# A hybrid trunk step on one core: unread products and another split order at the head, late state adds, output in one tensor, one output block by two products

## The chip, the cores and the metric

The kernel runs on one core of a Trainium2 chip. The metric is the device time of one execution in microseconds (us). Each kernel is run several times, and the median counts. The times and the profile are of the program as it runs on the chip; what the host does with the arrays before and after is not in them.

The engines are named as in the profile: PE is TensorE (the matrix products; PEld its weight loads), ACT is ScalarE, DVE is VectorE, POOL is GpSimd, and SP is SyncE, whose queue issues most of the DMAs.

## The reference

One layer (`DEPTH = 1`) of a model step for two request groups that share the weights: 256 new positions of a prompt and 32 positions of a running stream, 288 rows together, with 2048 features.

```python
def run_layer(...):
    xn = rmsnorm(x, norm_mix_pre)
    proj = xn @ w_in            # [u_pool 1024 | z 2048 | xBC 2560 | dt 32]
    pool = pool_mixer(u_pool)   # trailing means over 2, 4, 8, 16 positions
    ssd  = ssd_mixer(z, xBC, dt)  # causal conv, Mamba-2 scan, gate, norm; returns the new state
    x    = x + rmsnorm(concat[pool, ssd] @ w_out, norm_mix_post)
    h    = rmsnorm(x, norm_ffn_pre)
    up   = causal_dwconv3(h @ w_up)            # 2 * 5632 columns
    x    = x + rmsnorm((silu(gate) * value) @ w_down, norm_ffn_post)
```

The outputs are y for the prompt and for the sample, and for both groups the new pool history, the new conv histories and the new SSD state. The data type is fp32. A product with the unit matrix or with a diagonal matrix therefore stands for a copy or a scaling by rows.

## The kernel before

Activations lie with the features on the partitions: a tile is 128 features by 288 positions (`NT`; columns 0 to 255 are the prompt, 256 to 287 the sample). Every fp32 weight product is made of three faster products (`mm3`, L136 to L138): ACT copies a weight tile `raw` into a rounded `whi`, DVE subtracts it from `raw` and writes the remainder `wlo`; the activations are split in the same way (`xn`, `hn` and so on, by `split_from`, L99 on ACT and L100 on DVE). Weights come in by SP's queue, a few buffers ahead.

The order of the instructions comes from a scheduler that places the engines' queues. `keep_in_program_order` pins an instruction to its place in the program, `issue_after` sets it behind a given one, `high_priority` lets the fetches and splits run ahead.

The stages, in order of time:

- **The head** (L235 to L290). The first projection takes 16 k-steps of 128 input features with `w_first`, six output tiles (`acc` five times, `acc_x` once), 18 products a step. For each k the split `xn` of the input, `whi` (L270) and `wlo` (L271) are issued, and `input_squares` (L230 to L234) squares the input on ACT and sums it on POOL (`xsum`). The squares of several tiles go out in the later steps. At k = 13, `input_rstd` (L240) makes the mean over the features by a product with `mean` (a matrix filled with 1/2048), and `root` (L236) takes ACT's square root and DVE's reciprocal.
- **The projections, the SSD scan, the pool and the output projection.** `mix_out` (L660) reads each finished tile twice on ACT: `msq` (L668) the square for the norm, `mg` (L670) the scaled copy. Two last products `psum_m` (L745) end the norm's sum. Behind them come four pinned state updates: `state_s` for j = 3 and 2 (one product `psts`, ACT's copy `sx`, a POOL add into `sh`, L714, and the DMA to `new_ssd_s`), and `state_p` for j = 3 and 2 (two products `pst` each, L701).
- **The up loop** (L773 on). `residual` makes the tile x1[k] on DVE (`mg`, L764), `hn` is its split, and 7 output tiles take 21 products a k-step with `w_up1` (`whi` L798, `wlo` L799). From k = 4 on, the weight split is set behind the split of `hn` of the same k. DVE's work of this loop stands in one line (`in_line`). At k = 15, behind the second output tile, `psum_t` (L806) sums the squares for the next norm and `root` makes `r2`.
- **The feed-forward halves and the end.** Finished tiles of the last projection go through DRAM into rows of positions (`to_tokens`). The last 256 features come last and run in two parts (`run_a` for positions 128 to 287, `run_b` for 0 to 127). `fsq` (L960) are their squares, `psum_f` (L931 to L937) sums over the features, `final_rstd` (L943) takes the root `rf`, `turn` transposes the last tiles on PE. `y_out(q, b)` (L963) makes one block of 128 positions by 512 features of y on DVE: x = ft · rf + x, and writes it. Blocks with b = 1 are written first, then the sample's block `xr_s` (L1042, L1044), then the four blocks with b = 0, whose squares end last.

The sample's block lies in `xr_s` with the quarter q of the features on the partitions 32q to 32q + 31, and goes out as a pattern of 4 x 32 x 512:

```python
sp.dma_start(out=y_sample[0].rearrange("s (q c) -> q s c", q=4), in_=xr_s)
```

Of the kernel before, what the change touches and what calls it, by code (L numbers as in the profile page):

```python
# [43 lines left out]
def body(  # L44
# [16 lines left out]
    w_down,  # L61
    y_prompt,
    y_sample,
    new_pool,
# [180 lines left out]
    act.dma_start(out=g_mix_pre, in_=g0_in)  # L245
    input_tiles(0, 1)
    first = [acc_ps.tile([P, NT], F32, tag="acc", name="acc") if m < 5 else aux([P, NT], "acc_x") for m in range(6)]
    chunks = ((0, 1), (1, 1)) + tuple((k, 2) for k in range(2, KD, 2))
    x_with = {0: (1, 1), 1: (2, 2), 2: (4, 2), 4: (6, 3), 6: (9, 3), 8: (12, 4)}
    for kb, n in chunks:  # L250
        raw = wpool.tile([P, n, 768], F32, tag="raw", name="raw")
        sp.dma_start(out=raw, in_=w_first[:, kb : kb + n, :])
        if kb in x_with:
            input_tiles(*x_with[kb])
        if kb == 1:
            pool.dma_start(out=wdt, in_=w_dt)
        if kb == 2:
            pool.dma_start(out=par1, in_=par1_in)
            pool.dma_start(out=hp, in_=hp_in)
        if kb == 6:  # L260
            pool.dma_start(out=pc, in_=par2_in[:, :120])
            pool.dma_start(out=pf, in_=par2_in[:, 120:].rearrange("p (r t) -> p r t", r=6))
        for k in range(kb, kb + n):
            a = atile("xn")
            split_from(a, xT[:, k, :], g_mix_pre[:, k : k + 1])
            xn.append(a)
            hi, lo = wtile("hi", 1, 768)[:, 0, :], wtile("lo", 1, 768)[:, 0, :]
            step = 256 if k == 0 else 768
            for c in range(0, 768, step):
                act.activation(hi[:, c : c + step], raw[:, k - kb, c : c + step], AF.Copy)  # L270
                dve.tensor_tensor(  # L271
                    lo[:, c : c + step], raw[:, k - kb, c : c + step], hi[:, c : c + step].bitcast(F32), op=ALU.subtract
                )
# [434 lines left out]
    def state_s(j, x, h, pin=False):  # L708
        st = acc_ps.tile([P, 512], F32, tag="acc", name="psts")
        ins = pe.matmul(st, btok[:, j // 2, 2, :], x[:, 2, :], start=True, stop=True)  # L710
        if pin:
            tc.keep_in_program_order(ins)
        act.activation(x[:, 2, :], st, AF.Copy)
        pool.tensor_tensor(h, h, x[:, 2, :], op=ALU.add)  # L714
        sp.dma_start(out=new_ssd_s[:, 512 * j : 512 * j + 512], in_=h)

# [10 lines left out]
    for grp in ((0, 1), (2,), (3,), (4,), (5,), (6,), (7,)):  # L727
# [4 lines left out]
        if 2 <= grp[0] < 4:  # L732
            x_h = state_in(grp[0] - 2)
            state_p(grp[0] - 2, *x_h)
            state_s(grp[0] - 2, *x_h)
        elif 4 <= grp[0] < 6:
            late_in[grp[0] - 2] = state_in(grp[0] - 2)
# [6 lines left out]
    for i in range(2):  # L744
        tc.keep_in_program_order(pe.matmul(p_m, mean, last_sq[i], start=False, stop=i == 1))  # L745
    state_s(3, *late_in[3], pin=True)
    state_s(2, *late_in[2], pin=True)
    state_p(3, *late_in[3], pin=True)
# [23 lines left out]
    for k in range(KD):  # L772
# [190 lines left out]
    def y_out(q, b):  # L963
# [3 lines left out]
        for o, n, src in (  # L967
# [4 lines left out]
            if b:  # L972
                tc.keep_in_program_order(ins)
        sp.dma_start(out=y_prompt[0][b * P : (b + 1) * P, 512 * q : 512 * (q + 1)], in_=x)

# [67 lines left out]
    )  # L1043
    sp.dma_start(out=y_sample[0].rearrange("s (q c) -> q s c", q=4), in_=xr_s)  # L1044
# [12 lines left out]

_OUTS = [
    (1, 256, 2048), (1, 32, 2048), (P, 2, 15, NU), (P, 2, 3, NXC), (P, D_SSD), (P, D_SSD), (P, 2, 2, 2 * NF),
]  # L1060
# [72 lines left out]
```

## Time and profile before

| what | us |
|---|---|
| median of 3 runs | 1330.14 (1330.11 to 1331.14) |
| the profiled execution | 1329.91, span 1328.2 |
| PE busy | 1310.4 (99%) |
| DVE busy | 884.6 (67%) |
| ACT busy | 666.3 (50%) |
| POOL busy | 215.0 (16%) |
| mean granted TensorE clock | 0.997 |

The span runs from the first to the last instruction. Products are pipelined: the record of one lasts longer than the distance to the next. A row of the timeline gives the start, the busy time, the engine, the line, the operation, the tile written and the tiles read, the number of instructions in the row, and in brackets the idle time before it with the one who ended it. A row of the waits gives who waited for whom, the total, the number of times and the longest.

### The profile page before, as it was taken

The page shows a single profiled execution, that of the slowest core. Times are in us where ns is not written, and L with a number is a line of the kernel's source. Part 1 is how long each engine was busy: PE and PEld are TensorE (multiplying, and loading weights), DVE is VectorE, ACT ScalarE, POOL GpSimd, SP SyncE. Part 2 cuts the span into 40 slices and gives each one's busy share as a digit, 9 for nine tenths or more (in the row PEclk, how much of TensorE's full clock was granted, in tenths as well). Part 3 has the DMA queues.
Part 4 walks back from the last instruction along what each step waited for, and adds up shares of the span by engine and source line. Part 5 has one row for each costly group of instructions (what it writes and reads, how often), then busy time and mean ns, then how long its engine had stood idle before and what let it go on. Part 6 is the DMA issues. An engine that isn't in the chain of part 4 may idle for free.

```text
span 1328.2 us, 25077 instructions
## 1 busy us (share of the span) xinstructions
PE 1310.4 (99%) x10041; PEld 1295.1 (98%) x10041; DVE 884.6 (67%) x1460; ACT 666.3 (50%) x1002; POOL 215.0 (16%) x353
## 2 busy tenths in 40 slices
PE   7999999999999999999999999999999999999997
PEld 7999999999999989999999999999999999999996
DVE  8898998779644478977666643345666666664444
ACT  7558777446443455645445443334444444454442
POOL 6221102121211100211111100001111111101110
PEclk9999999999999999999999999999999999999998
DMA  7668884465666445666454454455444544566663
GB/s 287 230 194 255 287 242 160 140 240 206 232 206 207 147 143 195 199 188 185 164 183 162 151 175 161 160 180 177 172 159 164 186 159 159 175 235 175 209 181 93
DMA packets 104008, 249.81 MB, mean 188 GB/s; under 512 B 63748, under 2 KB 69444, under 8 KB 81492
## 3 DMA queue, kind: packets, MB, share of 16 engines
q1 hardware_dynamic: 101972, 243.11, 55.8%
q0 software_dynamic: 1488, 4.92, 1.1%
q8 instruction: 78, 1.28, 0.4%
q14 instruction: 38, 0.31, 0.1%
q10 hardware_dynamic: 432, 0.19, 0.1%
HBM read 236.23 MB, written 11.95 MB: 187 GB/s over the span
## 4 chain that ended last, share of the span: by engine, by line
PE 98%; DVE 1%; DMA 0%; ACT 0%; issue 0%; DVEq 0%; SPq 0%
PE acc L138 31%; PE acc L136 31%; PE acc L137 31%; PE acc_x L138 1%; PE acc_x L137 1%; PE acc_x L136 1%; PE py L467 1%; DVE xr L971 0%; PE run_a L1014 0%; PE low L1012 0%; DMA raw<-in_w_first 0%; PE py L469 0%; PE pst L701 0%; PE run_b L1027 0%; PE pdt L289 0%; DVE mg L764 0%
## 5 line engine op out<-in xcount | busy, mean ns | idle before, releaser
L131 DVE TENSOR_TENSOR wlo<-raw,whi 128x1024 fp32r<-128x1024 f32 (+1 forms) x386 | 464.0, 1203 | 334.7 <-ACT whi L130 332.5
L130 ACT ACTIVATE whi<-raw 128x1024 fp32r<-128x1024 f32 (+1 forms) x386 | 399.6, 1037 | 474.5 <-PE acc L137 382.9
L136 PE MATMUL acc<-hn,whi 128*128 128x288 f32 x1360 | 399.0, 294 | 0.1
L137 PE MATMUL acc<-hn,whi 128*128 128x288 f32 x1360 | 398.1, 293 | 0.0
L138 PE MATMUL acc<-hn,wlo 128*128 128x288 f32 x1360 | 397.7, 293 | 0.0
L136 PEld LDWEIGHTS acc<-hn,whi 128*128 128x128 f32 x1360 | 255.3, 188 | 0.9 <-ACT hn L778 0.9
L137 PEld LDWEIGHTS acc<-hn,whi 128*128 128x128 f32 x1360 | 255.3, 188 | 0.1
L138 PEld LDWEIGHTS acc<-hn,wlo 128*128 128x128 f32 x1360 | 255.2, 188 | 0.0
L136 PE MATMUL acc<-xn,whi 128*128 128x288 f32 x688 | 203.6, 297 | 5.7 <-ACT whi L270 5.7
L137 PE MATMUL acc<-xn,whi 128*128 128x288 f32 x688 | 200.6, 293 | 0.0
L138 PE MATMUL acc<-xn,wlo 128*128 128x288 f32 x688 | 198.6, 298 | 1.3 <-DVE wlo L271 1.3
L136 PE MATMUL acc<-fa,whi 128*128 128x288 f32 x660 | 194.0, 294 | 0.0
L137 PE MATMUL acc<-fa,whi 128*128 128x288 f32 x660 | 193.4, 293 | 0.0
L138 PE MATMUL acc<-fa,wlo 128*128 128x288 f32 x660 | 193.1, 293 | 0.0
L136 PEld LDWEIGHTS acc<-xn,whi 128*128 128x128 f32 x688 | 130.2, 189 | 6.6 <-ACT whi L270 5.7
L137 PEld LDWEIGHTS acc<-xn,whi 128*128 128x128 f32 x688 | 130.1, 189 | 0.2
L138 PEld LDWEIGHTS acc<-xn,wlo 128*128 128x128 f32 x688 | 127.8, 189 | 2.1 <-DVE wlo L271 1.5
L136 PEld LDWEIGHTS acc<-fa,whi 128*128 128x128 f32 x660 | 124.1, 188 | 0.0
L138 PEld LDWEIGHTS acc<-fa,wlo 128*128 128x128 f32 x660 | 123.9, 188 | 0.0
L137 PEld LDWEIGHTS acc<-fa,whi 128*128 128x128 f32 x660 | 123.9, 188 | 0.0
L825 POOL COPY fc_stage<-ebuf 128x4 f32<-128x4 f32 x88 | 27.2, 310 | 501.2 <-DVE ebuf L824 501.2
L831 DVE SCALAR_TENSOR_TENSOR fc<-ebuf,pf,fc 128x290 f32<-128x290 f32 x176 | 90.2, 518 | 2.9 <-ACT fc L829 0.3
(277 smaller groups left out, 1692.0 us busy)
## 6 DMA issues: line engine op xcount, KB each, us to landing
raw<-in_w_up SPq DMA_DIRECT2D x80, 1024.0 KB, 4.8
raw<-in_w_in SPq DMA_DIRECT2D x38, 1024.0 KB, 5.4
raw<-in_w_down SPq DMA_DIRECT2D x32, 1024.0 KB, 4.8
raw<-in_w_out SPq DMA_DIRECT2D x24, 1024.0 KB, 4.9
raw<-in_w_down SPq DMA_DIRECT2D x16, 768.0 KB, 4.3
raw<-in_w_up SPq DMA_DIRECT2D x8, 896.0 KB, 4.6
gb<-g_d SPq DMA_DIRECT2D x8, 832.0 KB, 6.4
raw<-in_w_first SPq DMA_DIRECT2D x7, 768.0 KB, 10.1
```

Of the source, the lines that this page charges most:

```text
L130: act.activation(hi, raw[:, k : k + n, :], AF.Copy)
L131: dve.tensor_tensor(lo, raw[:, k : k + n, :], hi.bitcast(F32), op=ALU.subtract)
L136: pe.matmul(out, wh, a[:, 0, :], start=start, stop=False)
L137: pe.matmul(out, wh, a[:, 1, :], start=False, stop=False)
L138: pe.matmul(out, wl, a[:, 0, :], start=False, stop=stop)
L467: pe.matmul(y[:, 0:256], xw[:, 0, c], m[:, j, 0:256], start=True, stop=False)
L825: pool.tensor_copy(fc_stage[:, :, :, i], e[:, 256:324].rearrange("p (s c) -> p s c", c=34)[:, :, 0:2])
L831: dve.scalar_tensor_tensor(c, e[:, r_ : r_ + 290], pf[:, r_, i : i + 1], c, op0=ALU.mult, op1=ALU.add)
```

## The change

Four places of the kernel change.

1. **The head.** Nine products `idle` (the matrix `mean` times itself, 128 x 128, fp32) stand pinned at PE's start; nothing reads them. The split `xn` of step k is set behind `whi` and `wlo` of step k - 2; the squares stand behind `whi` of step k - 1; the squares have four buffers instead of two; `input_rstd` comes at k = 14.
2. **The states.** For j = 3 and 2 `state_s` leaves out its POOL add and gives it back as a function. It is called on DVE, in the line of the up loop, at k = 4 and k = 5, and issues its output DMA there. For j = 0 and 1 it is called at once, on POOL as before.
3. **The up loop.** The weight split is set behind the split of `hn` from k = 3 on, instead of from k = 4.
4. **The tail.** All of y goes into one tensor `y_rows` of 128 x 9 x 512, with the sample as its ninth block, written as 128 rows of 512; the host lays the rows out again. The block q = 1, b = 0 is made on PE: the unit matrix times `xr[2]`, and behind it the diagonal matrix of `rf` (made by ACT) times `ft[2]`, into one PSUM tile, which ACT copies out. The other three stay with DVE.

```diff
-            q = xin.tile([P, NT], F32, tag="xsq", bufs=2, name="xsq")
+            q = xin.tile([P, NT], F32, tag="xsq", bufs=4, name="xsq")
...
     input_tiles(0, 1)
+    cut = []
+    idle = aux([P, P], "idle")
+    for i in range(9):
+        tc.keep_in_program_order(pe.matmul(idle, mean, mean, start=True, stop=True))
...
-            split_from(a, xT[:, k, :], g_mix_pre[:, k : k + 1])
+            with ExitStack() as order:
+                for ins in cut[k - 2] if k > 2 else ():
+                    order.enter_context(tc.issue_after(ins.ins))
+                split_from(a, xT[:, k, :], g_mix_pre[:, k : k + 1])
...
+            cut.append((w_hi, w_lo))
             for t in range(k - 1, k) if 0 < k < 9 else range(2 * k - 10, 2 * k - 8) if 8 < k < 13 else ():
-                input_squares(t)
-            if k == 13:
+                with tc.issue_after(cut[k - 1][0].ins):
+                    input_squares(t)
+            if k == 14:
                 input_rstd()
...
         act.activation(x[:, 2, :], st, AF.Copy)
-        pool.tensor_tensor(h, h, x[:, 2, :], op=ALU.add)
-        sp.dma_start(out=new_ssd_s[:, 512 * j : 512 * j + 512], in_=h)
+
+        def add(eng=pool):
+            ins = eng.tensor_tensor(h, h, x[:, 2, :], op=ALU.add)
+            sp.dma_start(out=new_ssd_s[:, 512 * j : 512 * j + 512], in_=h)
+            return ins
+
+        return add
...
-    state_s(3, *late_in[3], pin=True)
-    state_s(2, *late_in[2], pin=True)
+    late_add = [state_s(j, *late_in[j], pin=True) for j in (3, 2)]
...
+        if 3 < k < 6:
+            in_line(late_add[k - 4], dve)
         hn.append(a)
...
-            if k > 3:
+            if k > 2:
                 order.enter_context(tc.issue_after(hi.ins))
                 order.enter_context(tc.issue_after(lo.ins))
...
-        sp.dma_start(out=y_prompt[0][b * P : (b + 1) * P, 512 * q : 512 * (q + 1)], in_=x)
+        sp.dma_start(out=y_rows[:, 4 * b + q, :], in_=x)
...
-    sp.dma_start(out=y_sample[0].rearrange("s (q c) -> q s c", q=4), in_=xr_s)
+    sp.dma_start(out=y_rows[:, 8, :], in_=xr_s)
...
-    for j in range(2):
-        feature_sums(fsq[j], 1, False, j == 1)
+    y_ps = acc_ps.tile([P, 512], F32, tag="acc", name="y_ps")
+    feature_sums(fsq[0], 1, False, False)
+    tc.keep_in_program_order(pe.matmul(y_ps, ident, xr[2], start=True, stop=False))
+    feature_sums(fsq[1], 1, False, True)
...
-    for q in range(4):
+    diag = fp.tile([P, NT], F32, tag="fr", bufs=2, name="diag")[:, :P]
+    act.activation(diag, ident, AF.Copy, scale=rf[:, 0:1])
+    pe.matmul(y_ps, diag, ft[2], start=False, stop=True)
+    act.activation(xr[2], y_ps, AF.Copy)
+    for q in (0, 2, 3):
         y_out(q, 0)
+    sp.dma_start(out=y_rows[:, 1, :], in_=xr[2])
```

Three places of the order show what moves. Line numbers of the changed kernel differ by a few from those of the kernel before (L270 is its L276, L271 its L277). First DVE in the head, from `wlo` of k = 2 on, before; `wlo` is the remainder of a weight tile, `xn` that of an input tile:

```order
L271 TENSOR_TENSOR wlo_240<-raw_203,whi_239 128x768
L100 SCALAR_TENSOR_TENSOR xn_267<-xT_130,g0_125,xn_267 128x288
L100 SCALAR_TENSOR_TENSOR xn_295<-xT_130,g0_125,xn_295 128x288
L271 TENSOR_TENSOR wlo_271<-raw_264,whi_270 128x768
L271 TENSOR_TENSOR wlo_299<-raw_264,whi_298 128x768
L100 SCALAR_TENSOR_TENSOR xn_328<-xT_130,g0_125,xn_328 128x288
L100 SCALAR_TENSOR_TENSOR xn_356<-xT_130,g0_125,xn_356 128x288
L100 SCALAR_TENSOR_TENSOR xn_387<-xT_130,g0_125,xn_387 128x288
L100 SCALAR_TENSOR_TENSOR xn_415<-xT_130,g0_125,xn_415 128x288
L100 SCALAR_TENSOR_TENSOR xn_448<-xT_130,g0_125,xn_448 128x288
L100 SCALAR_TENSOR_TENSOR xn_479<-xT_130,g0_125,xn_479 128x288
L271 TENSOR_TENSOR wlo_332<-raw_323,whi_331 128x768
```

And the same place of the changed kernel:

```order
L277 TENSOR_TENSOR wlo_250<-raw_213,whi_249 128x768
L99 SCALAR_TENSOR_TENSOR xn_277<-xT_130,g0_125,xn_277 128x288
L99 SCALAR_TENSOR_TENSOR xn_305<-xT_130,g0_125,xn_305 128x288
L277 TENSOR_TENSOR wlo_281<-raw_274,whi_280 128x768
L277 TENSOR_TENSOR wlo_309<-raw_274,whi_308 128x768
L99 SCALAR_TENSOR_TENSOR xn_338<-xT_130,g0_125,xn_338 128x288
L99 SCALAR_TENSOR_TENSOR xn_366<-xT_130,g0_125,xn_366 128x288
L277 TENSOR_TENSOR wlo_342<-raw_333,whi_341 128x768
L277 TENSOR_TENSOR wlo_370<-raw_333,whi_369 128x768
```

Six `xn` in a row have become two, with the next two `wlo` behind them.

Second PE at the end of the up loop, around `psum_t`, before (`acc` and `acc_x` are PSUM tiles of output; the first `acc_x` with `hn_5813` belongs to the next weight):

```order
L138 MATMUL acc_5803<-hn_6320,wlo_6327 128x288
L806 MATMUL psum_t_5801<-xsum_3583,mean_84 128x288
L136 MATMUL acc_5804<-hn_6320,whi_6326 128x288
...
L138 MATMUL acc_5808<-hn_6320,wlo_6327 128x288
L136 MATMUL acc_x_6432<-hn_5813,whi_6435 128x288
L137 MATMUL acc_x_6432<-hn_5813,whi_6435 128x288
```

And after, where the 15 products between them (five tiles, three each) stand ahead of `psum_t`:

```order
L137 MATMUL acc_5813<-hn_6330,wlo_6337 128x288
L137 MATMUL acc_5814<-hn_6330,wlo_6337 128x288
L820 MATMUL psum_t_5807<-xsum_3593,mean_84 128x288
L135 MATMUL acc_x_6442<-hn_5819,whi_6445 128x288
L136 MATMUL acc_x_6442<-hn_5819,whi_6445 128x288
```

So `psum_t` is now the last instruction of the loop on PE, and the next weight's first product its neighbour.

Third ACT at the end of the output projection, before (`msq` is the square of a finished tile, `rm` the root of its norm, `whi` a weight split):

```order
L798 ACTIVATE whi<-raw 128x896 x3
L668 ACTIVATE msq_3581<-acc 128x288
L670 ACTIVATE mg<-acc,par_119 128x288
L798 ACTIVATE whi<-raw 128x896
L668 ACTIVATE msq_3582<-acc 128x288
L670 ACTIVATE mg<-acc,par_119 128x288
L237 ACTIVATE rm<-psum_m,eps_t 128x288
```

And after:

```order
L812 ACTIVATE whi<-raw 128x896 x3
L676 ACTIVATE msq_3591<-acc 128x288
L678 ACTIVATE mg<-acc,par_119 128x288
L676 ACTIVATE msq_3592<-acc 128x288
L678 ACTIVATE mg<-acc,par_119 128x288
L236 ACTIVATE rm<-psum_m,eps_t 128x288
```

The fourth `whi`, which stood between the two tiles, is gone from there.

More of the change, by code (lines that the diff above doesn't have):

```diff
@@ L61, in body @@
     w_down,
-    y_prompt,
-    y_sample,
+    y_rows,
     new_pool,
@@ L269, in body @@
             for c in range(0, 768, step):
-                act.activation(hi[:, c : c + step], raw[:, k - kb, c : c + step], AF.Copy)
-                dve.tensor_tensor(
+                w_hi = act.activation(hi[:, c : c + step], raw[:, k - kb, c : c + step], AF.Copy)
+                w_lo = dve.tensor_tensor(
                     lo[:, c : c + step], raw[:, k - kb, c : c + step], hi[:, c : c + step].bitcast(F32), op=ALU.subtract
                 )
+            cut.append((w_hi, w_lo))
             for t in range(k - 1, k) if 0 < k < 9 else range(2 * k - 10, 2 * k - 8) if 8 < k < 13 else ():
-                input_squares(t)
-            if k == 13:
+                with tc.issue_after(cut[k - 1][0].ins):
+                    input_squares(t)
+            if k == 14:
                 input_rstd()
@@ L734, in body @@
             state_p(grp[0] - 2, *x_h)
-            state_s(grp[0] - 2, *x_h)
+            state_s(grp[0] - 2, *x_h)()
         elif 4 <= grp[0] < 6:
@@ L1052, in body @@
         turn(j, 1)
-    for q in range(4):
+    diag = fp.tile([P, NT], F32, tag="fr", bufs=2, name="diag")[:, :P]
[3 more added lines that the diff above has]
+    for q in (0, 2, 3):
         y_out(q, 0)
+    sp.dma_start(out=y_rows[:, 1, :], in_=xr[2])
     ffn.close()
 _OUTS = [
-    (1, 256, 2048), (1, 32, 2048), (P, 2, 15, NU), (P, 2, 3, NXC), (P, D_SSD), (P, D_SSD), (P, 2, 2, 2 * NF),
+    (P, 9, 512), (P, 2, 15, NU), (P, 2, 3, NXC), (P, D_SSD), (P, D_SSD), (P, 2, 2, 2 * NF),
 ]
@@ L1119 @@
     r = _run(nc, [arrays], core_ids=[0])
-    y_p, y_s, n_pool, n_sconv, h_p, h_s, n_fconv = (_np.asarray(r.results[0][f"out_{i}"]) for i in range(len(_OUTS)))
+    y, n_pool, n_sconv, h_p, h_s, n_fconv = (_np.asarray(r.results[0][f"out_{i}"]) for i in range(len(_OUTS)))
     def rows(a, s):
@@ L1127, in heads @@
         return _np.ascontiguousarray(a.T).reshape(1, 1, HEADS, 64, P)
+    y_p = _np.ascontiguousarray(y[:, :8].reshape(P, 2, D_MODEL).transpose(1, 0, 2)).reshape(1, NP_, D_MODEL)
+    y_s = _np.ascontiguousarray(y[:, 8].reshape(4, NS, 512).transpose(1, 0, 2)).reshape(1, NS, D_MODEL)
     return (
```

## The prediction

> **What bounds the kernel now.** I read the page's busy shares first, then TensorE's waits, then the timeline at each place that those waits point to, and last the windows of the end, where TensorE no longer works.
>
> ```profile
> span 1328.2 us, 25077 instructions
> PE 1310.4 (99%) x10041; PEld 1295.1 (98%) x10041; DVE 884.6 (67%) x1460; ACT 666.3 (50%) x1002; POOL 215.0 (16%) x353
> PE acc L136 <- ACT whi L270: 5.7, 1, 5.7
> PE acc L138 <- DVE wlo L271: 1.3, 1, 1.3
> PE psum_f L931 <- ACT fsq L960: 0.8, 1, 0.8
> PE psum_m L745 <- ACT msq L668: 0.7, 1, 0.7
> ```
>
> TensorE (PE) is busy for 1310.4 of 1328.2 us, so an edit can win only in the 17.8 us left: 5.7 before the first product, 1.3 in the first projection, 0.7 at the end of the mixer's output projection, and the end behind the last products, from 1318.3 on, of which the 0.8 is the beginning. The products themselves may also run slower than they can. The timeline of PE's first 30 us shows that they do:
>
> ```profile
> 5.71 0.61 PE L136 MATMUL acc<-xn,whi 128*128 128x288 f32 x1 [5.71 <-ACT whi L270]
> 6.36 0.44 PE L136 MATMUL acc<-xn,whi 128*128 128x288 f32 x1
> 10.68 0.35 PE L136 MATMUL acc<-xn,whi 128*128 128x288 f32 x1
> 11.00 0.30 PE L136 MATMUL acc<-xn,whi 128*128 128x288 f32 x1
> 12.86 0.29 PE L136 MATMUL acc<-xn,whi 128*128 128x288 f32 x1
> 15.25 0.29 PE L136 MATMUL acc<-xn,whi 128*128 128x288 f32 x1
> 30.25 0.94 PE L138 MATMUL acc<-xn,wlo 128*128 128x288 f32 x5 [1.30 <-DVE wlo L271]
> ```
>
> A k-step of the first projection is 18 products. The two steps k=0 and k=1 take from 5.71 to 12.86, 7.15 us; k=2, from 12.86 to 15.25, takes 2.39. One record lasts 0.44 us before 10.68 and 0.30 from 11.00 on: about 5.1 us after the first product the array doubles its speed.
>
> **The change part by part.** First the head. The nine products `idle` need only `mean`, which a memset fills in the first microsecond; their price is that of an fp32 product of 128 columns:
>
> ```profile
> 112.46 0.22 PE pcb L422 x2
> 10.42 1.58 ACT L270 ACTIVATE whi<-raw 128x768 fp32r<-128x768 f32 x2 [1.47 <-DMA raw<-in_w_first]
> ```
>
> 0.22 us at full speed, 0.44 at half, nine of them 4.0 us: from about 1.3 to 5.3, inside the 5.7 us in which PE waits anyway. They cost nothing as long as `whi` is ready no earlier than 5.3. Their effect can only be on the speed. If the array's slow time counts from the first product of any kind, it ends 5.1 us after 1.3, at about 6.4, not 10.8. Then k=0 and k=1 take 2 x 2.39 = 4.8 and end at about 10.6, and the next limit is the data: `whi` of k=2 waits for its transfer until 10.42 and the first of the two is done at 10.42 + 0.79 = 11.2. So k=2 begins at about 11.3, not 12.86: 1.55 us won. As that limit leaves 0.7 spare, the speed may come up to 1.5 us late (about 7.8) before this shrinks. If the half-microsecond gap behind the nine starts the count again, the gain is nil: the bounds are 0 and 1.55, and I take 1.55, since PE would have been busy 4.0 of the 4.5 us before 5.71.
>
> The Trainium skill's page "TensorE: Matmul & The Clock Gate", Part 1, states that the array runs at half clock by default and at full clock after a busy window of about 3.4 us, and that these windows run freely, so that the moment varies from run to run. The 5.1 us here agree with it (between one window and two). By that rule, as an estimate, full speed comes between 4.7 and 8.1, and this term is 1.3 to 1.55.
>
> The other half of the head is the order of the splits. VectorE (DVE) has no idle time there:
>
> ```profile
> 20.00:25.00 5.00, 5.00 (x40) 5.00 (x39) 5.00 (x5) 4.42 (x10) 3.76 (x5) 1.00 0.83 340
> 15.64 2.42 DVE L271 TENSOR_TENSOR wlo<-raw,whi 128x768 fp32r<-128x768 f32 x2
> 17.98 4.32 DVE L100 SCALAR_TENSOR_TENSOR xn<-xT,g,xn 128x288 fp32r<-128x288 f32 x6
> 18.47 1.38 ACT L99 ACTIVATE xn<-xT,g 128x288 fp32r<-128x288 f32 x3
> 28.64 5.63 DVE L271 TENSOR_TENSOR wlo<-raw,whi 128x768 fp32r<-128x768 f32 x5
> ```
>
> Six `xn` remainders (4.32 us) stand in one piece, for steps far ahead, while the `wlo` that PE needs next wait behind them: that is the 1.30 at 30.25. The new order gives two `wlo`, two `xn`, and so on. One step then costs DVE 1.21 + 0.72 = 1.93 us against PE's 2.39, so the stall should go: 1.30 won. What is late next is the same queue with GpSimd's sums beside it, 0 to 0.3 us given back by the spread of those durations. The later `input_rstd` needs only ScalarE (ACT) and DVE and is wanted by the X projection's evacuations tens of products later: nothing.
>
> The middle: the end of the output projection and the states.
>
> ```profile
> 475.28 0.95 ACT L798 ACTIVATE whi<-raw 128x896 fp32r<-128x896 f32 x1 [0.63 <-PE acc L137]
> 476.13 0.39 ACT L668 ACTIVATE msq<-acc 128x288 f32<-128x288 f32 x1
> 476.58 0.75 PE L745 MATMUL psum_m<-msq,mean 128*128 128x288 f32 x2 [0.72 <-ACT msq L668]
> 478.88 3.60 PE L701 MATMUL pst<-sx,btok 128*128 128x512 f32 x8
> 478.90 2.71 POOL L714 TENSOR_TENSOR sh<-sh,sx 128x512 f32<-128x512 f32 x2 [20.01 <-ACT sx L713]
> 480.52 1.41 DVE L764 TENSOR_TENSOR mg<-mg,xT 128x288 f32<-128x288 f32 x1
> ```
>
> The weight split of k=3 (0.95) sits on ACT just ahead of the last `msq`, for which PE waits 0.72. With `k > 2` it comes later: 0.72 won, as ACT had been idle for 0.63 ahead of that split. The two GpSimd adds (2.71) slow the residual's add `mg` to 1.41 beside them, but PE works through the pinned state products until 482.5, so taking them away wins at most the 0.1 us that is left there. On DVE the two adds cost about 0.8 us each (1.21 x 512/768), and `wlo` of k=3 joins them (1.21 x 896/768 = 1.4): 3.0 us in the first steps of the up loop, where the waits above show none of PE for DVE. I put them at nothing; with no cover they cost 3.0. Their two output DMAs now stand behind those adds in SyncE's (SP's) queue, ahead of two `w_up1` fetches that are not needed for some ten microseconds.
>
> One wait is added that the diff does not show. At the end of that loop 15 products used to stand between `psum_t` and the first product of the next weight; now that product follows at once, and its PSUM buffer is the one that ACT must first read for the root `r`:
>
> ```profile
> 524.92 0.65 PE L806 MATMUL psum_t<-xsum,mean 128*128 128x288 f32 x2
> 525.61 0.50 ACT L237 ACTIVATE r<-psum_t,eps_t 128x288 f32<-128x288 f32 x1 [0.35 <-PE psum_t L806]
> ```
>
> The stream of `psum_t` ends near 525.4, the root at 526.11: 0.7 to 0.8 us in which PE now stands still; 0.76 lost. Everything on PE is queued behind it. Bounds: 0 if the next product gets another buffer, 1.8 if one more weight split (0.95 x 1024/896 = 1.1) still runs on ACT ahead of the root.
>
> The tail:
>
> ```profile
> 1318.33 0.38 PE L931 MATMUL psum_f<-mean,fsq 128*128 128x1 f32 x2 [0.76 <-ACT fsq L960]
> 1318.62 0.70 SPq L1044 DMA_DIRECT2D out<-xr_s  x1
> 1319.24 2.47 DVE L971 SCALAR_TENSOR_TENSOR xr<-ft,rf,xr 128x512 f32<-128x512 f32 x4
> 1320.02 4.14 SPq L974 DMA_DIRECT2D out<-xr  x4
> L974 SPq DMA_DIRECT2D out<-xr x8: 332/342/1668, 1315.3 to 1322.9; - x8
> DMA to landing us min/median/max: 2.0/3.2/5.3
> 1320.00:1321.50 1.50, 0.00 (x0) 0.00 (x0) 1.50 (x3) 0.00 (x0) 0.00 (x0) 1.00 0.25 22
> 1323.00:1324.00 1.00, 0.00 (x0) 0.00 (x0) 0.00 (x0) 0.00 (x0) 0.00 (x0) 0.50 0.93 350
> 1325.50:1326.50 1.00, 0.00 (x0) 0.00 (x0) 0.00 (x0) 0.00 (x0) 0.00 (x0) 0.50 0.26 100
> 1327.20:1328.20 1.00, 0.00 (x0) 0.00 (x0) 0.00 (x0) 0.00 (x0) 0.00 (x0) 0.50 0.00 0
> 480.80 0.60 ACT L705 ACTIVATE ho<-pst 128x512 f32<-128x512 f32 x1 [1.12 <-PE pst L701]
> ```
>
> In the windows the last two numbers are the DMA engines' busy share and GB/s. While the sample's block `xr_s` is under way alone (1320.0 to 1321.5) a quarter of the 16 engines is busy, at 22 GB/s; after the others have finished (1325.5) again a quarter, at 100. So that one write holds four engines from 1319.6 to 1327.2, the four blocks behind it land 4 to 5 us after issue instead of 2.0, and two of SP's issues take over a microsecond instead of 0.34. Written as 128 rows of 512, like the others, it should be gone by 1320.4, before the first block. Then: first block issued at 1320.02, landed at 1322.0; three more at 256 KB / 350 to 390 GB/s = 0.67 to 0.75 behind it: 1324.1; the last 1.0 of the span stays: 1325.0, against 1328.2. 3.2 won, with 2.9 to 3.6 by those rates.
>
> The same section needs the third block in time. DVE has one block less, so it ends at 1321.45, not 1322.11. The block q=1 is two fp32 products of 512 columns, each two passes of 3.60 / 8 = 0.45: 0.9. The first runs in the 0.76 us in which PE waits at 1318.33, so it may push `psum_f` by 0 to 0.15. Behind the root and reciprocal (1319.2) come the diagonal on ACT (128 columns, under 0.60), 0.9 of product and 0.60 of copy: about 1321.3, before DVE's last block. Without the cheaper write, this alone would save the 0.66 of one DVE block.
>
> The Trainium skill's page "DMA: Bandwidth & Descriptors", section "Why a DMA increments its semaphore by 16 and not by 1", has a transfer use the largest number of engines up to 16 that divides the slowest dimension of both patterns: four for 4x32x512, sixteen for 128x512. The quarter share agrees; by that rule the whole 3.2 falls due.
>
> Sum: -1.55 - 1.30 - 0.72 + 0.76 - 3.2 = -6.0. The profiled execution took 1329.91 us, 1.7 more than its span, and lies 0.2 below the median of the runs, 1330.14. So the span becomes 1322.2, and the median 1324.1.
>
> **The rivals.** *The nine products do not bring the speed forward.* The gap of half a microsecond behind them, or products of this kind, do not count. For it: in before, 1.7 us of work ahead of 7.4 were not enough. Against it: PE would be busy almost all the time from 1.3. Then the term of 1.55 goes: 1325.7.
>
> *The sample's write is not what holds the end,* or stays slow in its new form, because its rows and not their number are slow (22 GB/s is little even for four engines). Then only 0.66 of the tail is won: 1326.6. With both rivals: 1328.2.
>
> *The head becomes a chain,* and the kernel slower. The splits of step k are now tied behind the weight halves of k-2 on both engines. If they are taken strictly one after another, a step costs 0.79 (`whi`) + 1.21 (`wlo`) + 0.46 + 0.72 (`xn`) = 3.18 us against 2.39 on PE, over twelve steps 9.5 more, with both gains of the head gone: 1330.1 - 3.2 - 0.7 + 0.8 + 9.5 = 1336.5. It decides from 2.65 us a step on (12 x 0.26 eats the other 3.2). Against it: the tie orders each engine's queue, and in that order ACT need not wait for DVE; each engine alone needs less than 2.39.
>
> **How the numbers follow.** The forecast as summed has 0.62, the first rival 0.17, the second 0.10, both 0.04, the chain 0.05; 0.02 is for what I did not see. The range runs from the sum with the tail's best rate, no root wait and nothing given back (1330.1 - 1.55 - 1.3 - 0.8 - 3.6 = 1322.9) up past both single rivals, with the 0.3 and 1.0 that the head and the root may give back: 1322.9 to 1327.6. A measurement of this kernel tells about 0.2% from no change, 2.7 us. Faster than 1327.5 are the forecast, the first rival and nearly all of the second, less a little for their unknown costs: 0.85. Within are both rivals together and the rest of the second: 0.08. Slower: 0.07.
>
> **What would show it.** Right: in the timeline, `idle` from about 1.3 to 5.3 and records of 0.30 us already for k=0 or k=1; k=2 near 11.3; no wait of PE for `wlo` L271; none for `msq`; one new wait of 0.7 to 0.8 of the first `acc_x` behind `psum_t`, for ACT's root; in the windows of the end a DMA share near 1 from the first block to the last, no stretch at a quarter, and under 6 us from the last reciprocal to the end. Wrong: 0.44 us records up to 10.8; a share of a quarter behind the last block; PE waiting in the up loop's first steps for DVE; a new wait on fetches of weights.

## The result, and the profile after

The changed kernel takes 1324.39 us (median of 5 runs, 1323.95 to 1324.51), the kernel before 1330.12 us in the same comparison (5 runs, 1330.04 to 1331.14). The ratio is 0.9954, with a 95% interval of 0.9941 to 0.9967. The forecast was 1324.1, with a range of 1322.9 to 1327.6. The profiled execution's span is 1322.7 us, 5.5 less than before; the sum had 6.0.

The page and TensorE's waits (who waits for whom, total, number, longest) answer to the first rows of the prediction:

```profile
span 1322.7 us, 25123 instructions
PE 1314.2 (99%) x10063; PEld 1297.7 (98%) x10063; DVE 882.8 (67%) x1461; ACT 667.3 (50%) x1004; POOL 221.9 (17%) x351
PE acc L135 <- ACT whi L276: 1.6, 2, 1.4
PE idle L249 <- POOL mean L182: 1.2, 1, 1.2
PE y_ps L1071 <- ACT diag L1070: 0.6, 1, 0.6
PE acc_x L135 <- ACT r L236: 0.6, 1, 0.6
```

The waits for `wlo` and for `msq` are gone. The forecast wait for the root `r` is there. A wait of 1.4 for a `whi` in the head is new, and the head's timeline shows which:

```profile
1.21 4.02 PE L249 MATMUL idle<-mean 128*128 128x128 f32 x18 [1.21 <-POOL mean L182]
5.49 0.40 PE L135 MATMUL acc<-xn,whi 128*128 128x288 f32 x1 [0.26 <-ACT whi L276]
11.93 0.40 PE L135 MATMUL acc<-xn,whi 128*128 128x288 f32 x1 [1.39 <-ACT whi L276]
11.03 1.58 ACT L276 ACTIVATE whi<-raw 128x768 fp32r<-128x768 f32 x2 [1.46 <-DMA raw<-in_w_first]
```

The nine products (18 passes) fill 1.21 to 5.23, and the first useful one runs at full speed. k=0 and k=1 are done by 10.6, as forecast, and then PE stands still until the weights of k=2 are there. Their `whi` starts on ACT at 11.03, 0.6 later than in the trace before; this moment is called the arrival below.

The tail in SP's queue, in two windows of the end (last two numbers: DMA share and GB/s), and in the row of all writes of y:

```profile
1316.15 0.33 SPq L1058 DMA_DIRECT2D out<-xr_s  x1
1317.55 0.99 SPq L988 DMA_DIRECT2D out<-xr  x2
1319.01 0.33 SPq L1075 DMA_DIRECT2D out<-xr  x1
1319.43 0.41 SPq L988 DMA_DIRECT2D out<-xr  x1
1320.00:1321.00 1.00, 0.00 (x0) 0.00 (x0) 0.00 (x0) 0.00 (x0) 0.00 (x0) 0.50 1.02 387
1321.50:1322.70 1.20, 0.00 (x0) 0.00 (x0) 0.00 (x0) 0.00 (x0) 0.00 (x0) 0.50 0.00 0
DMA to landing us min/median/max: 2.0/2.0/2.3
```

Every block lands 2.0 to 2.3 us after its issue, where the blocks before took up to 5.3, and behind the last block there is no stretch at a quarter of the engines any more.

Where the 5.5 us came from, read at the same product in both timelines:

| place | forecast | measured |
|---|---|---|
| head: speed and stall, up to `prs`, the product of `input_rstd` that makes the mean | 1.55 + 1.30 | 2.33 |
| projections and SSD | 0 | 0.31 |
| `msq` ahead of `psum_m` | 0.72 | 0.71 |
| start of the up loop | 0 to 0.1 | 0.33 |
| wait for the root `r` behind `psum_t` | -0.76 | -0.86 |
| the up loop's other products | 0 | -0.36 |
| tail, from the last `psum_f` to the end | 3.2 | 3.03 |
| sum | 6.0 | 5.5 |

The 0.31 of the second row arises at one place, the `py` products of the SSD scan. Most of it stands ahead of the first of them, which starts 0.42 us after the product ahead of it in the trace before, and 0.23 in the changed kernel. Why is open. The same place shows 1.32 in a second execution of the old order (`b_sample_128` below), so with the old order it scatters by 0.9 us.

### The profile page after: what moved, and what is told of

Same layout as the page of the kernel before. It is cut to its first block, busy times and chain, and to the rows that moved or that the text cites. A ratio compares the mean times of both kernels' runs of the same rounds, so it can differ in the third digit from the quotient of the medians.

```text
span 1322.7 us, 25123 instructions
## 1 busy us (share of the span) xinstructions
PE 1314.2 (99%) x10063; PEld 1297.7 (98%) x10063; DVE 882.8 (67%) x1461; ACT 667.3 (50%) x1004; POOL 221.9 (17%) x351
## 4 chain that ended last, share of the span: by engine, by line
PE 99%; DMA 1%; ACT 0%; SPq 0%; issue 0%; DVE 0%
PE acc L135 31%; PE acc L137 31%; PE acc L136 31%; PE acc_x L135 1%; PE acc_x L137 1%; PE py L475 1%; PE acc_x L136 1%; DMA raw<-in_w_first 1%; PE pst L709 1%; PE run_a L1028 0%; PE low L1026 0%; PE run_b L1041 0%; PE py L477 0%; PE psts L718 0%; PE pdt L297 0%; PE py L481 0%
## 5 line engine op out<-in xcount | busy, mean ns | idle before, releaser
L135 PE MATMUL acc<-hn,whi 128*128 128x288 f32 x1360 | 394.3, 294 | 0.0
L136 PE MATMUL acc<-hn,whi 128*128 128x288 f32 x1360 | 393.4, 293 | 0.0
L137 PE MATMUL acc<-hn,wlo 128*128 128x288 f32 x1360 | 392.5, 293 | 0.0
L137 PE MATMUL acc<-xn,wlo 128*128 128x288 f32 x688 | 195.0, 295 | 0.0
```

The lines of the kernel that those rows point to most:

```text
L135: pe.matmul(out, wh, a[:, 0, :], start=start, stop=False)
L136: pe.matmul(out, wh, a[:, 1, :], start=False, stop=False)
L137: pe.matmul(out, wl, a[:, 0, :], start=False, stop=stop)
```

## The experiments

All are edits of the changed kernel, but one; times are medians of 5 to 11 runs, to be held against its 1324.39. The kernel before, run beside them, lay at 1330.12, 1330.16 and 1331.0 in the three comparisons. The changed kernel itself was not run again in them, so where two medians differ by less than about half a us, the traces have to decide.

**The sample's write.** The first attempt meant to give the write its old pattern.

```diff
-    sp.dma_start(out=y_rows[:, 8, :], in_=xr_s)
+    sp.dma_start(out=y_rows[:, 8, :].rearrange("(q s) c -> q s c", q=4), in_=xr_s)
```

> The changed kernel with the sample's block written into the same place of y_rows, but as a pattern of 4 x 32 x 512. Theory (the pattern decides how many DMA engines take it): a quarter of the engines busy while it is alone and at the end, blocks behind it land 4 to 5 us after issue, the end 2.4 to 3.2 us later: 1326.8 to 1327.6. Rival (the old destination, rows of 8 KB apart in an array of its own, was slow): the share of DMA stays near 1 and the time within 0.3 us of 1324.4.

1324.31 us, the same span to the tenth, but this decides nothing: the four quarters lie behind one another in `y_rows`, so the pattern covers the same 128 rows in the same order, and in the trace nothing changed: SP's issue still takes 0.33. It serves as a repeat of the changed kernel: the medians agree within 0.1 us. The next one puts the rows in another order, so that the pattern is no longer the same as 128 rows one behind the other:

```diff
+    sp.dma_start(out=y_rows[:, 8, :].rearrange("(s q) c -> q s c", q=4), in_=xr_s)
```

> The changed kernel with the sample's block written into y_rows in another order of its rows (4s + q instead of 32q + s; the host reads them so), so that the pattern stays 4 x 32 x 512. Theory (the pattern decides how many DMA engines take it): SP's issue takes 0.7 us again, a quarter of the engines busy while it is alone and at the end, the blocks behind it land 4 to 5 us after issue, the end 2.4 to 3.2 us later: 1326.8 to 1327.6. Rival (the old destination was slow, a separate array with rows of 8 KB): share near 1, within 0.3 us of 1324.4.

1327.09 us (1326.75 to 1327.44), 2.7 more. SP's queue, two windows, and the landing of y's writes:

```profile
1315.54 0.70 SPq L1058 DMA_DIRECT2D out<-xr_s  x1
1316.93 2.33 SPq L988 DMA_DIRECT2D out<-xr  x2
1316.50:1318.00 1.50, 1.12 (x2) 0.30 (x2) 1.50 (x4) 0.28 (x2) 0.00 (x0) 1.00 0.23 20
1323.00:1324.00 1.00, 0.00 (x0) 0.00 (x0) 0.00 (x0) 0.00 (x0) 0.00 (x0) 0.50 0.15 55
DMA to landing us min/median/max: 2.0/3.1/5.3
```

All signs of the old tail are back in the new tensor: an issue of 0.70, a quarter of the engines at 20 GB/s, 5.3 to landing. From the last `psum_f` to the end it takes 9.87 us, against 6.84 in the changed kernel and 9.87 in the kernel before. And the one edit alone, in the kernel before:

```diff
-    sp.dma_start(out=y_sample[0].rearrange("s (q c) -> q s c", q=4), in_=xr_s)
+    sp.dma_start(out=y_sample, in_=xr_s)   # y_sample is now 128 x 512
```

> The kernel before with one edit: the sample's block goes to an array of 128 rows of 512 as a pattern of 128 x 512. Theory: this alone brings the tail's gain, blocks land 2.0 to 2.3 us after issue, 2.6 to 3.1 us faster than before: 1327.0 to 1327.5. Rival (all of y in one tensor, or the block by products, is what counts): under 0.7 us faster.

1327.02 us (1326.47 to 1328.34), 3.1 less than the kernel before (1330.16 there; ratio 0.9975, 0.9966 to 0.9984). From `psum_f` to the end: 6.80. So the pattern is the whole of the tail's gain, and neither the one tensor nor the block by products is needed for it. The Trainium skill's page "DMA: Bandwidth & Descriptors", section "Why a DMA increments its semaphore by 16 and not by 1", lets the largest divisor up to 16 of both slowest dimensions set the number of engines, which is 4 for one pattern and 16 for the other. The share of 0.23 agrees.

**The block by products.** All four last blocks on DVE:

```diff
...
-    pe.matmul(y_ps, diag, ft[2], start=False, stop=True)
-    act.activation(xr[2], y_ps, AF.Copy)
-    for q in (0, 2, 3):
+    for q in range(4):
         y_out(q, 0)
...
```

> The changed kernel with all four last blocks on DVE and none by products. Theory of the prediction (one DVE block less is 0.66 us off the end): 0.66 us slower, 1325.0. Rival, from the trace after (the block by products is ready at the same moment as DVE's last, and SP issues the two one after the other): DVE's last block ends 0.66 us later but is issued at once, so the last issue moves by 0.2 to 0.3 us only, 1324.6 to 1324.7.

1324.39 us: no difference. The tail takes 6.80 us from `psum_f`, against 6.84. DVE ends 0.66 later, but SP then has a steady row of issues, while in the changed kernel the block by products and DVE's last are ready at the same moment and queue at SP (1319.01 and 1319.43 above).

**The unread products.** None of them, then four:

```diff
-    idle = aux([P, P], "idle")
-    for i in range(9):
-        tc.keep_in_program_order(pe.matmul(idle, mean, mean, start=True, stop=True))
```

> The changed kernel without the nine unread products; all else stays. Theory (they only bring the doubled product speed forward): records of 0.44 us until about 5 us after the first product, k=2 of the first projection begins at 12.6 to 12.9 us instead of 11.93, and the kernel takes 0.7 to 1.0 us more, about 1325.2. Rival (k=2 is held by the arrival of its weights in any case, and the splits' order alone made the gain of the head): k=2 stays within 0.3 us of 11.93 and the time within 0.3 us of 1324.4.

1324.82 us (1324.36 to 1325.27), span 1323.6: 0.4 more by the medians, less than the 0.7 to 1.0 expected.

```diff
-    for i in range(9):
+    for i in range(4):
```

> The changed kernel with four unread products instead of nine; they end near 2.9 us, and PE then waits 2.6 us for its first weights. Theory (the speed follows how busy PE has been over a window of a few us): the doubled speed comes 4 to 6 us after the first useful product, as without any, about 1324.8. Rival (the first product of any kind starts the count): it comes 2.8 to 5 us after the first unread one, by 6.3, as with nine, 1324.4.

1324.66 us (1324.00 to 1324.78), span 1323.0. The switch of the speed in both timelines, first without, then with four:

```profile
5.51 0.61 PE L135 MATMUL acc<-xn,whi 128*128 128x288 f32 x1 [5.51 <-ACT whi L273]
11.20 0.36 PE L136 MATMUL acc<-xn,whi 128*128 128x288 f32 x1
11.40 0.30 PE L135 MATMUL acc<-xn,whi 128*128 128x288 f32 x1
```

```profile
1.21 2.08 PE L249 MATMUL idle<-mean 128*128 128x128 f32 x8 [1.21 <-POOL mean L182]
5.49 0.61 PE L135 MATMUL acc<-xn,whi 128*128 128x288 f32 x1 [2.20 <-ACT whi L276]
9.97 0.33 PE L135 MATMUL acc<-xn,whi 128*128 128x288 f32 x1
10.13 0.30 PE L136 MATMUL acc<-xn,whi 128*128 128x288 f32 x1
```

The moment of the switch is read here as the start of the first product whose distance to the next is the short one. With four products and a gap of 2.2 us it comes 4.6 us after the first useful product and 8.9 after the first unread one, so the rival that the first product of any kind starts a count falls. Whether the four shorten the slow time a little is open: without any, it lasted 5.2, 5.7 and 5.9 us in three executions. With nine, in ten executions, the switch came between 4.27 and 7.03 us, that is 3.1 to 5.8 us after the first unread product. That is early enough each time, since 7.8 would have done. The Trainium skill's page "TensorE: Matmul & The Clock Gate", Part 1, speaks of busy windows of about 3.4 us that run freely, and of a moment that varies by 500 ns either way. The spread of 2.8 us here is far more than that, though less than one such window; and twice the switch came only 3.1 us after the first product.

The medians differ by only 0.3 and 0.4 us because another quantity scatters more: the arrival of the weights of k=2. The start of that `whi` on ACT, and of the mean's product `prs` behind the head, in the traces with the new order of the splits:

| kernel | `whi` of k=2 | `prs` | difference |
|---|---|---|---|
| changed | 11.03 | 40.71 | 29.68 |
| all blocks on DVE | 10.75 | 40.38 | 29.63 |
| state adds on POOL (below) | 10.14 | 39.80 | 29.66 |
| `psum_t` early (below) | 10.45 | 40.12 | 29.67 |
| four unread products | 9.99 | 40.98 | 30.99 |
| none | 10.97 | 41.55 | 30.58 |

With nine products and the new order the head runs at a fixed distance from that arrival (29.63 to 29.78 in nine executions), and the arrival lies between 10.14 and 11.08. With four or none it loses 0.9 to 1.3 us against it. At the arrival of the trace before, 10.42, the head's gain would have been 2.9, not 2.33. A trace with the old head bears this out: `b_sample_128` had its weights at 11.00, and the head of the changed kernel, with 11.03, ends 2.9 earlier.

**The order of the splits.** First all of the head's order back, with the nine products kept; then only the tie of the `xn` removed.

```diff
-            q = xin.tile([P, NT], F32, tag="xsq", bufs=4, name="xsq")
+            q = xin.tile([P, NT], F32, tag="xsq", bufs=2, name="xsq")
...
-                for ins in cut[k - 2] if k > 2 else ():
+                for ins in ():
...
-                with tc.issue_after(cut[k - 1][0].ins):
-                    input_squares(t)
-            if k == 14:
+                input_squares(t)
+            if k == 13:
```

> The changed kernel with the head's splits, squares, their two buffers and input_rstd ordered as before, but with the nine products. Theory (six xn remainders ahead of wlo made PE wait): DVE again does xn in runs of four to six, PE waits for a wlo of the first projection, and since PE now reaches that place about 0.9 us earlier while DVE does not, it waits 1.3 to 2.2 us: 1325.7 to 1326.6. Rival (the wait was an accident of one execution's data arrival): no wait of PE for wlo over 0.3 us, within 0.3 us of 1324.4.

1328.24 us (1327.04 to 1328.81), 3.9 more, where 1.3 to 2.2 were expected. The second keeps the squares' place, their four buffers and k = 14:

```diff
-                for ins in cut[k - 2] if k > 2 else ():
+                for ins in ():
```

> The changed kernel with the xn splits free again (no tie to the weight halves of two steps earlier); the squares keep their place and their four buffers. Theory (the xn running ahead is the whole of the head's stall): DVE does four to six xn in a row, PE waits 1.3 us or more for a wlo, and the time is near that of the run with the whole old order, 1327.0 to 1328.2. Rival (the two buffers of the squares, by which ACT's next whi waits for POOL, are the larger part): 1325.0 to 1326.0.

1324.45 us (1323.79 to 1325.88): no difference, so both the theory and its rival missed. PE's waits in the head, and the rows of ACT, DVE and POOL that lead to them, with the whole old order:

```profile
22.70 0.40 PE L135 MATMUL acc<-xn,whi 128*128 128x288 f32 x1 [1.11 <-ACT whi L276]
30.68 0.93 PE L137 MATMUL acc<-xn,wlo 128*128 128x288 f32 x5 [1.36 <-DVE wlo L277]
21.47 0.44 ACT L232 ACTIVATE xsq<-xT 128x288 f32<-128x288 f32 x1 [0.54 <-POOL xsum L233]
21.82 1.56 ACT L276 ACTIVATE whi<-raw 128x768 fp32r<-128x768 f32 x2
18.42 4.30 DVE L99 SCALAR_TENSOR_TENSOR xn<-xT,g,xn 128x288 fp32r<-128x288 f32 x6
22.68 3.02 DVE L277 TENSOR_TENSOR wlo<-raw,whi 128x768 fp32r<-128x768 f32 x2
25.61 3.54 DVE L99 SCALAR_TENSOR_TENSOR xn<-xT,g,xn 128x288 fp32r<-128x288 f32 x4
19.36 4.03 POOL L233 TENSOR_TENSOR xsum<-xsum,xsq 128x288 f32<-128x288 f32 x4
```

And with the free `xn` alone:

```profile
11.05 0.40 PE L135 MATMUL acc<-xn,whi 128*128 128x288 f32 x1 [0.42 <-ACT whi L276]
19.24 1.57 ACT L276 ACTIVATE whi<-raw 128x768 fp32r<-128x768 f32 x2
17.14 3.76 DVE L99 SCALAR_TENSOR_TENSOR xn<-xT,g,xn 128x288 fp32r<-128x288 f32 x6
20.83 1.82 DVE L277 TENSOR_TENSOR wlo<-raw,whi 128x768 fp32r<-128x768 f32 x2
22.57 2.92 DVE L99 SCALAR_TENSOR_TENSOR xn<-xT,g,xn 128x288 fp32r<-128x288 f32 x4
17.23 2.08 POOL L233 TENSOR_TENSOR xsum<-xsum,xsq 128x288 f32<-128x288 f32 x2
```

DVE does six `xn` in a row in both, and from the `wlo` of k=2 to that of k=8 it does the same twenty operations in the same order, without idle time. With the old order they take 18.9 us, as they do in the two traces with the old head of the kernel before; with the free `xn` alone they take 15.9. The difference is in how long single operations last. An `xn` takes 0.51 or about 1.06 us, a `wlo` 0.95 or about 1.55, and in all fourteen traces the long times are found only where POOL adds a square into `xsum` meanwhile. With the old order twelve such adds start before the `wlo` of k=8 does, and twelve of the twenty operations are long; in the run with the free `xn` it is seven and seven. So the `wlo` of k=8, for which PE waits at 30.68, is late because DVE was slowed; its `whi` had been ready since 26.8.

The wait at 22.70 has another cause, and stands on ACT: in the old order a square goes ahead of the `whi` of k=6 and waits 0.54 until POOL has added an earlier one and its buffer is free. So that `whi` starts at 21.82 instead of 19.24.

In the traces, the run with the old order is 2.8 us behind the changed kernel by the end of the head (at an arrival 0.17 us earlier). Another 1.5 come in the SSD stage, where PE waits 0.7 at issue ahead of the first `py` and 0.3 for a `wlo`; the first of these is the place that scatters with the old order. Which of the three things that differ between the two runs (place of the squares, buffers, k = 14) does it was not tried apart. The tie of the `xn` was not tried with the squares in their old place either.

**The late adds.** On POOL again, right behind the state products:

```diff
-    late_add = [state_s(j, *late_in[j], pin=True) for j in (3, 2)]
+    for j in (3, 2):
+        state_s(j, *late_in[j], pin=True)()
...
-        if 3 < k < 6:
-            in_line(late_add[k - 4], dve)
```

> The changed kernel with the two late state adds on POOL again, right behind the state products. In its order the up loop's products stand in threes (two with whi, one with wlo, tile by tile) as before the change, and two products, not none, stand between psum_t and the next weight's first. Theory of the traces: mg is slow beside POOL again and the up loop starts 0.3 us later, but the products' spacing goes back from 132.8 to 131.1 ns (336 products, 0.4 to 0.5 us) and the wait for the root shrinks by 0.26: 1324.0, no slower than 1324.4. Rival (the prediction's: the adds on DVE are hidden, those on POOL cost 0.1, the order of products costs nothing): 1324.5 to 1324.7.

1324.32 us (1323.60 to 1324.69): no difference, and as a sum, not because nothing happened. The up loop's second product comes 0.90 us after the last `pst` began, 0.56 in the changed kernel. The wait for the root is 0.3 less. The products did not go back to 131.1 ns (132.7), and their order is a mixture and not tile by tile; that part of the expectation missed. Measured from the first late `psts` to the first product of the down projection, the two differ by 0.03 us. So the second part of the change is worth nothing here: it wins 0.3 at the loop's start, and with the order that the scheduler makes of it the wait at `psum_t` is as much longer.

**The weight split of k = 3.**

```diff
-            if k > 2:
+            if k > 3:
```

> The changed kernel with the weight split of k = 3 where it was, ahead of the last msq. Theory (ACT does it just when msq could run): PE waits 0.7 us for msq again, and the time is 0.5 to 0.8 us more, 1324.9 to 1325.2, with the products of the up loop's first steps in threes again, which gives back up to 0.2. Rival (the wait is made up for behind, by the pinned state products): within 0.2 us of 1324.4.

1326.47 us, more than the 1324.9 to 1325.2 expected, but its runs scatter over 3 us (1325.07 to 1328.32), so the trace has to say more than the time. It is of a run of 1325.40; what made the longer ones longer is not shown. PE waits 0.7 for `msq` again, and 0.92 instead of 0.59 for the root; up to the first `psts` it loses 0.70 against the changed kernel, at the tail it is 0.9 late. The rival that the pinned products make it up falls.

**The root, and the products' order.** `psum_t` ahead of the last five tiles again:

```diff
+            with ExitStack() as order:
+                if k == KD - 1 and m > 1:
+                    order.enter_context(tc.issue_after(root_at.ins))   # root_at: the product psum_t
+                mm3(up1[m], whi[:, c], wlo[:, c], a, k == 0, k == KD - 1)
...
```

> The changed kernel with the last five tiles' products of k = 15 set behind psum_t, so that 15 products stand between it and the next weight's first, as in the kernel before. Theory (the added wait is the root's): the wait of acc_x for r goes, 0.7 to 0.9 us faster, 1323.5 to 1323.7. Rival (psum_t then waits for the sum of squares, which ACT makes behind weight splits): PE waits at psum_t instead, within 0.3 us of 1324.4.

1323.45 us (1323.08 to 1323.71), 0.9 less. The changed kernel's rows, and those of this one:

```profile
523.58 0.65 PE L820 MATMUL psum_t<-xsum,mean 128*128 128x288 f32 x2
524.81 0.40 PE L135 MATMUL acc_x<-hn,whi 128*128 128x288 f32 x1 [0.59 <-ACT r L236]
```

```profile
520.98 0.65 PE L823 MATMUL psum_t<-xsum,mean 128*128 128x288 f32 x2
521.25 0.51 PE L135 MATMUL acc<-hn,whi 128*128 128x288 f32 x1
```

No wait is left, and `psum_t` does not wait for its sum. The second step pins the up loop's products tile by tile:

```diff
...
+                for w, b, s in ((wh, 0, k == 0), (wh, 1, False), (wl, 0, False)):
+                    ins = pe.matmul(up1[m], w, a[:, b, :], start=s, stop=k == KD - 1 and w is wl)
+                    if k > 2:
+                        tc.keep_in_program_order(ins)
```

> The changed kernel with psum_t ahead of the last five tiles (as in e_root_early) and the up loop's products pinned tile by tile (whi, whi, wlo) from k = 3 on. Theory (the spacing of the products depends on their order; the wlo halves are ready 1.8 us before their step begins in any case): spacing back from 132.7 to 131.1 ns over 270 products, 0.4 us faster than e_root_early, 1323.0 to 1323.2. Rival (the spacing differs for another reason, or the pinned products wait for wlo or for the sum of squares): no faster than e_root_early, 1323.4 or more.

1323.08 us (1322.89 to 1323.21), the fastest of all: 0.9941 of the kernel before (0.9929 to 0.9954), with 1.3 us off the changed kernel by the medians. Five k-steps (105 products) in the kernel before, the changed one and this one:

```profile
502.05 0.29 PE L136 MATMUL acc<-hn,whi 128*128 128x288 f32 x1
515.81 0.29 PE L136 MATMUL acc<-hn,whi 128*128 128x288 f32 x1
```

```profile
498.47 0.30 PE L135 MATMUL acc<-hn,whi 128*128 128x288 f32 x1
512.42 0.43 PE L135 MATMUL acc<-hn,whi 128*128 128x288 f32 x2
```

```profile
498.22 0.42 PE L821 MATMUL acc<-hn,whi 128*128 128x288 f32 x2
511.98 0.42 PE L821 MATMUL acc<-hn,whi 128*128 128x288 f32 x2
```

13.76, 13.95 and 13.76 us: 131.0, 132.9 and 131.0 ns a product. In this stretch of the changed kernel each k-step runs through its seven output tiles three times (first half of the split `hn` with `whi`, second half with `whi`, then with `wlo`); in the other two, all three products of a tile follow one another. From the first late `psts` to the down projection this kernel is 0.40 us shorter than the one without the pins, as much as the medians differ.

## Why the prediction was right, and where it was not

The time came within 0.3 us of the forecast, and most terms hold by themselves, not only in their sum. That it came so close is partly luck: 0.5 too little in the head and 0.36 lost in the up loop, which the sum did not have, stand against 0.3 in the SSD scan and 0.3 at the loop's start, which it did not have either.

- *The speed.* Right in what bounds it: the switch came early enough, and k=2 begins when its weights arrive. The term was mis-sized: k=2 began 0.93 us earlier, not 1.55, since I took 10.42 for the arrival from one execution, as if it were fixed. It is the head's largest scatter, 9.99 to 11.08, and this execution had it late. Without the nine products the trace is 0.85 longer and the median 0.4. The condition that the slow time counts from the first product of any kind does not hold in general: four products and a gap did not bring the switch forward to match.
- *The stall of 1.30.* It went, and the sum had its size right, but the reason given was wrong, so the size was luck. That six `xn` stand in one piece is no cause by itself: with the `xn` free and the squares in their new place they still do, without the stall. What held the `wlo` was that DVE's operations ran long beside POOL's adds of the squares. The rows of the prediction had the sign of it: six `xn` in 4.32 us are 0.72 each, where an undisturbed one takes 0.51 in the same trace, and it named the slow `mg` beside POOL's adds in the middle of the kernel, but counted POOL's sums in the head only as up to 0.3 given back. This account is read from the traces; no run moved POOL's adds alone. In the changed kernel, undoing the tie of `xn` to `cut` costs nothing.
- *`msq`.* Right: 0.72 forecast, 0.71 measured, and its undoing costs 0.7.
- *The states.* The adds on DVE are hidden, as said. Their removal from POOL won 0.33 at the loop's start and not 0.1, because the first product also came 0.2 us late behind the last `pst`, within what the page counts as busy.
- *The wait that the diff does not show.* Right in place and nearly in size: 0.76 forecast, 0.86 measured (the profile counts 0.59 of it as a wait), 0.9 won back by moving the product.
- *The up loop's products.* Missed: 0.36 us, with no wait anywhere. The sum has no term for the order of the loop's products, though the listing of the change shows two `wlo` products in a row where there were threes.
- *The tail.* Right: 3.2 forecast, 3.03 measured, and the pattern is all of it. The fallback, that the block by products alone would save 0.66, was not tried in the old tail; in the new one it saves nothing.

Of the rivals, that the unread products do not count has fallen, though four of them are too few and all nine are worth less than was forecast; that the write is not what holds the end has fallen in both directions; the chain in the head did not appear: with the tie of the `xn` and without it the time is the same.

## What to carry to other kernels

A write whose outer dimension was 4 held a quarter of the engines here, and everything that queued behind it; where an end waits for writes, look at the share of DMA engines first, and try a pattern of 128 rows. When a wait names an engine that was busy all along, compare how long the same operation takes at different times, and look at what the other engines do meanwhile; then test each tie alone before crediting it. And after a local edit look at the scheduler's order in places that the diff does not touch: here it took back 1.2 us of what the edits had won, and moving one product and pinning the order of one loop won it back.

## What the runs showed of the hardware

- The spacing of identical products followed their order. Tile by tile (`whi`, `whi`, `wlo` into one PSUM tile) they follow every 131.0 ns, in passes over seven tiles every 132.9, with the same tile shapes and no idle time between. Why is open.
- One write of 4 x 32 x 512 moves at 20 to 22 GB/s on its quarter of the engines while it is alone, much less than a quarter of the 387 GB/s that all sixteen reach, and at 55 to 100 GB/s in a window of 1 us near its end. What slows its first microseconds was not tried.
- The switch to full speed came 3.1 to 5.8 us after the first product in ten executions with the same nine products ahead, and 5.2 to 5.9 us after it in three without any.
- In the head, an `xn` on DVE takes 0.51 us and a `wlo` of 768 columns 0.95; beside POOL's adds of the squares many take about 1.06 and 1.55. No long one was found without such an add, among 37 `xn` and 91 `wlo` that ran clear of them.
- The granted clock reads 1.00 from the start, also while products are spaced at half speed; only at the end, 2.4 us after PE's last product in the kernel before and 0.7 in the changed one, does it fall to 0.50.
